# Low parts of the memories' weights moved from VectorE to GpSimd in a hybrid encoder

## The chip, the cores and the metric

One Trainium2 chip, of which the kernel uses one core. The metric is the device time of one execution in microseconds (us). The engines are named as the profile names them: PE is TensorE (PEld its weight loads), DVE is VectorE, ACT is ScalarE, POOL is GpSimd, SP is SyncE, whose queue issues the DMAs here.

## The reference

One layer of an encoder, on a prompt of 1024 tokens and a sample of 2048 tokens, each with 256 memory tokens, model width 1024, all in float32.

```python
h = rms_norm(x, norm_pre)
z = jnp.einsum('btd,de->bte', h, w_in)          # 1024 -> 2304, split into eight parts
pool_out = multiscale_pool(u_pool, pool_w, pool_scale) * silu(g_pool)
attn_out = block_self_attention(rope(rms_norm(q)), rope(rms_norm(k)), v) * silu(g_attn)
mh = rms_norm(mem, mem_norm)
kv_m = jnp.einsum('bmd,de->bme', mh, w_mem_kv)  # 1024 -> 512: keys and values of the memories
x_out = memory_attention(q_x, k_m, v_m) * silu(g_x)
y = jnp.einsum('bte,ed->btd', concatenate([pool_out, attn_out, x_out]), w_out)
return x + rms_norm(y, norm_post)
```

## The kernel before

The kernel has two stretches. In the first (about 700 us) all projections are made; in the second come the attention, the output projection and the norms, in an order of slots written out by hand. The change is in the first stretch, at its very start.

**How a product is made.** A float32 matrix is split into a high part (a copy rounded to the format that PE takes, written by ACT, line 68) and a low part (the rest, a subtraction, line 69, on DVE before the change). Each product of a 128-row chunk is three matmuls, in `product`: high by high (L548), high by low (L549) and low by high (L550), summed over eight chunks of the 1024 inputs into one PSUM tile `pz` (a ring of four). The trace prints the two operands of a matmul in either order.

**The rows.** `hT_block` takes 512 rows of the memories or of x in four tiles of 128 rows: load `x` (L508, a ring of four tiles), sum of squares on ACT (L515), the reciprocal root `rs` in two steps, a small one on DVE (L61) and a power on POOL (L63), then DVE scales the rows by `rs` and the norm's gains (L517), PE transposes them in two groups of four (L523, into `pt`, a ring of two PSUM tiles), and ACT and DVE split each group into `hT_hi` and `hT_lo` (L68, L69). A `pt` tile is free again when its `hT_lo` is written.

**The weights.** `weights` loads a piece of a weight matrix into `wraw` (L539), of which there is **one** buffer, and splits it into `w_hi` and `w_lo` (rings of two). The next piece's load can start only when both parts of the one before are written. The first three uses are: `w_mem_kv` for the memories' values in two halves of 128x1024 (tiles numbered 251 to 253 in the order listings), `w_mem_kv` for their keys, 128x2048 (260 to 262), and then the pieces of `w_in`, 128x3072 each (474 to 476, then 636 to 638).

**The groups in order.** `mem_v` (the memories' values; `pz_362` to `pz_446`), `mem_k` (their keys; `pz_480` and `pz_511`, matmuls of 128x512; the results are scaled and split on DVE and ACT into `qxst`, one buffer), then the token groups, first `group_n1` (`pz_661` and on, matmuls of 128x384, with norms and rotary positions on POOL and DVE). Before that, `rope_tables` makes four tables of 128x1024 on POOL (L595, with small copies, L587), which `group_n1` needs.

**The order of the work.** In this stretch the instructions of each engine are put in order when the program is built, by a scheduler with its own timeline; at run time each engine goes through its list in order and waits at whatever isn't ready. A change of one instruction's engine therefore moves many others in the lists, while the work stays the same.

Of the kernel before, what the change touches and what calls it, by code (L numbers as in the profile page):

```python
# [7 lines left out]
F32 = mybir.dt.float32  # L8
F32R = mybir.dt.float32r
AF = mybir.ActivationFunctionType  # L10
ALU = mybir.AluOpType
# [12 lines left out]
def encoder(ctx, tc, I, O):  # L24


    nc = tc.nc
# [35 lines left out]
        nc.gpsimd.tensor_tensor(out=r, in0=r, in1=mhalf[:, 0:n], op=ALU.pow)  # L63
        return r

    def split(hi, lo, src):

        nc.scalar.copy(out=hi, in_=src)  # L68
        nc.vector.tensor_tensor(out=lo, in0=src, in1=hi.bitcast(F32), op=ALU.subtract)  # L69


    KA, KB, V = [], [], []
# [60 lines left out]
    class Group:  # L133
# [78 lines left out]
        def weights(self, k, j):  # L212
            if j == 0:
                self.P[k] = dbl.tile([128, 2, 512], F32, name="P", tag="P", bufs=6)
            S = pss.tile([128, 512], F32, name="S", tag="S")
            keys = slice(128 * k, 128 * k + 128)
            for n, (K, q) in enumerate(((KA, self.qa[:, j]), (KB, self.qb[0:65, j]))):
                rows_ = slice(0, 128 if n == 0 else 65)
                if self.kind < 2:
                    nc.tensor.matmul(S, lhsT=K[self.kind][rows_, keys], rhs=q, start=n == 0, stop=n == 1)  # L220
                    continue
                for i in range(2):
                    x = slice(256 * i, 256 * i + 256)
                    nc.tensor.matmul(S[:, x], lhsT=K[2][rows_, i, j, keys], rhs=q[:, x],
                                     start=(n, i) == (0, 0), stop=(n, i) == (1, 1),
                                     skip_group_check=True)
            nc.scalar.activation(out=self.P[k][:, j], in_=S, func=AF.Exp)  # L227
# [209 lines left out]
    for g in groups:  # L437
        n, c = first[g], g.chunks
# [14 lines left out]
    looks, n = {}, len(slots)  # L453
# [22 lines left out]
    with ExitStack() as p1:  # L476
# [24 lines left out]
        def hT_block(sb, blk):  # L501

            kind = SB[sb][0]
            hi = big.tile([128, NC, 512], F32R, name="hT_hi", tag="hT_hi")
            lo = big.tile([128, NC, 512], F32R, name="hT_lo", tag="hT_lo")
            for i in range(4):
                x = ftwo.tile([128, D], F32, name="x", tag="x", bufs=4)
                nc.sync.dma_start(out=x, in_=rows(sb, blk, i))  # L508
                if kind not in gains:
                    gains[kind] = fone.tile([128, D], F32, name="gain", tag="gain")  # L510
                    src = I["mem_norm" if kind == "mem" else "norm_pre"]
                    nc.sync.dma_start(out=gains[kind], in_=src.broadcast_to([128, D]))
                junk = fone.tile([128, D], mybir.dt.bfloat16, name="junk", tag="junk")
                ss = ftwo.tile([128, 1], F32, name="ss", tag="ss")
                nc.scalar.activation(out=junk, in_=x, func=AF.Square, accum_out=ss)  # L515
                r = rsqrt(ftwo, ss, 1, D, "rsx")
                nc.vector.scalar_tensor_tensor(out=x, in0=x, scalar=r[:, 0:1], in1=gains[kind],  # L517
                                               op0=ALU.mult, op1=ALU.mult)
                for half in range(2):
                    pt = pst.tile([128, 4, 128], F32, name="pt", tag="pt")  # L520
                    for c in range(4):
                        cc = 4 * half + c
                        nc.tensor.transpose(out=pt[:, c], in_=x[:, 128 * cc:128 * cc + 128],  # L523
                                            identity=ident)
                    cs = slice(4 * half, 4 * half + 4)
                    split(hi[:, cs, 128 * i:128 * i + 128], lo[:, cs, 128 * i:128 * i + 128], pt)
            return hi, lo

        def weights(src, pieces, cuts=1):

            n = sum(w for _, w in pieces)
            raw = big.tile([128, NC, 384], F32, name="wraw", tag="wraw", bufs=1)
            hi = big.tile([128, NC, 384], F32R, name="w_hi", tag="w_hi")
            lo = big.tile([128, NC, 384], F32R, name="w_lo", tag="w_lo")
            for q in range(cuts):
                cs, at = slice(NC // cuts * q, NC // cuts * (q + 1)), 0
                for start, w in pieces:
                    cols = src[:, start:start + w].rearrange("(c p) f -> p c f", p=128)
                    nc.sync.dma_start(out=raw[:, cs, at:at + w], in_=cols[:, cs])  # L539
                    at += w  # L540
                split(hi[:, cs, 0:n], lo[:, cs, 0:n], raw[:, cs, 0:n])
            return hi, lo

        def product(ps, terms, beside=lambda: None):
# [93 lines left out]
        def heads_transposed(src, npair):  # L638

            pt = pst.tile([128, 4, 128], F32, name="ptq", tag="ptq")  # L640
            for c in range(npair):
                nc.tensor.transpose(out=pt[:, c], in_=src[:, 128 * c:128 * c + 128], identity=ident)
            o = ftwo.tile([128, 2, 3, 128], F32R, name="qst", tag="qst")
            split(o[:, 0, 0:npair], o[:, 1, 0:npair], pt[:, 0:npair])
            return o
# [140 lines left out]
        w_mem = I["w_mem_kv"][0]  # L786
# [27 lines left out]
        def first_weights(sb):  # L814
            src, pieces, _ = groups_of(sb)[0]
            return weights(src, pieces, cuts=2 if sb == 0 else 1)
# [6 lines left out]
        for sb, (kind, s, nb, b0) in enumerate(SB):  # L823
            groups = groups_of(sb)
            nxt = []
            for gi, (src, pieces, run) in enumerate(groups):
                w = nxt_w
                if gi + 1 < len(groups):
                    nxt_w = weights(groups[gi + 1][0], groups[gi + 1][1])
                elif sb + 1 < len(SB):  # L830
                    nxt_w = first_weights(sb + 1)
                final = gi + 1 == len(groups)
                last = sb + 1 == len(SB)
                if last and gi == 3:
                    front.close()
                    early = ctx.enter_context(tc.tile_pool(name="early", bufs=1, side="right", reuse_waits="tile"))
                    open_early()
                    for g in loads.pop(-1):
                        g.load()
                if last and gi == 3:  # L840
                    heads.close()
                    psn = ctx.enter_context(tc.tile_pool(name="psn", bufs=2, space=PSUM, side="right", reuse_waits="tile"))
                for blk in range(nb):
                    if kind == "mem" and gi == 0 and blk == 0:
                        nxt.append(hT_block(sb + 1, 0))
                    if last and final:
                        with tc.manual_schedule(engines={mybir.EngineType.PE}):
                            run(s, b0 + blk, cur[blk], w, look_ahead)
                    else:
                        run(s, b0 + blk, cur[blk], w)  # L850
                    if final and sb + 1 < len(SB) and len(nxt) < SB[sb + 1][2]:
                        nxt.append(hT_block(sb + 1, len(nxt)))
# [22 lines left out]
    with tc.manual_schedule(engines=order):  # L875
        slot = 0
        while slot < len(slots) or later or fill:
# [14 lines left out]
            n = -(-(len(fill) - pauses) // max(1, until[0] - slot - pauses)) if fill else 0  # L892
            for _ in range(n):
# [3 lines left out]
                out, h, c, start, final = x  # L897
# [57 lines left out]
```

## Time and profile before

| what | value |
|---|---|
| time, median of 3 runs (lowest to highest) | 1884.36 us (1883.71 to 1887.12) |
| the profiled execution: its own time, its span | 1885.09 us, 1883.0 us |
| PE busy | 1816.8 us, 96% of the span |
| DVE, ACT, POOL busy | 1131.4, 697.3, 856.7 us (60%, 37%, 45%) |
| DMA | 181.83 MB, mean 97 GB/s |

The span runs from the first to the last instruction of the profile; the time of the execution has 2.09 us more around it. A row of a timeline has the start and the duration in us, the engine, the line and operation, output<-inputs, the shapes, how many instructions are merged (x2), and in brackets the idle time before it with what ended it. The starts of pipelined instructions lie a little ahead of the ends of those before them.

### The profile page before, as it was taken

The page shows a single profiled execution, that of the slowest core. Times are in us where ns is not written, and L with a number is a line of the kernel's source. Part 1 is how long each engine was busy: PE and PEld are TensorE (multiplying, and loading weights), DVE is VectorE, ACT ScalarE, POOL GpSimd, SP SyncE. Part 2 cuts the span into 40 slices and gives each one's busy share as a digit, 9 for nine tenths or more (in the row PEclk, how much of TensorE's full clock was granted, in tenths as well). Part 3 has the DMA queues.
Part 4 walks back from the last instruction along what each step waited for, and adds up shares of the span by engine and source line. Part 5 has one row for each costly group of instructions (what it writes and reads, how often), then busy time and mean ns, then how long its engine had stood idle before and what let it go on. Part 6 is the DMA issues. An engine that isn't in the chain of part 4 may idle for free. (4 is left out here: it accounts for less than half of the span.)

```text
span 1883.0 us, 23531 instructions
## 1 busy us (share of the span) xinstructions
PE 1816.8 (96%) x8520; PEld 1282.0 (68%) x8520; DVE 1131.4 (60%) x1304; ACT 697.3 (37%) x1266; POOL 856.7 (45%) x756
## 2 busy tenths in 40 slices
PE   7999999999999998999999999999999999999996
PEld 6888888988988874465564656556565656565564
DVE  7755146431545167867768676767868576756743
ACT  5523233222422115434434343444434343433331
POOL 3665017520546008845638374664837461413313
PEclk9999999999999999999999999999999999999998
DMA  7634454254433926212122220212222242223211
GB/s 243 201 113 121 109 160 132 76 162 110 116 113 102 216 70 167 68 30 79 46 79 62 70 64 25 79 45 79 62 74 62 67 132 64 91 84 100 86 40 62
DMA packets 148485, 181.83 MB, mean 97 GB/s; under 512 B 21505, under 2 KB 118417, under 8 KB 148369
## 3 DMA queue, kind: packets, MB, share of 16 engines
q1 hardware_dynamic: 148368, 180.33, 33.6%
q8 instruction: 67, 1.10, 0.3%
q14 instruction: 50, 0.40, 0.1%
HBM read 126.50 MB, written 53.62 MB: 96 GB/s over the span
## 5 line engine op out<-in xcount | busy, mean ns | idle before, releaser
L227 ACT ACTIVATE P<-S 128x512 f32<-128x512 f32 x688 | 399.3, 598 | 558.3 <-PE S L220 436.2
L194 DVE TENSOR_REDUCE nb<-N 128x1 f32<-128x1024 f32 x256 | 311.6, 1218 | 240.3 <-PE N L191 239.5
L239 POOL TENSOR_TENSOR z<-z,P 128x512 f32<-128x512 f32 x224 | 316.9, 1415 | 223.7 <-ACT P L227 218.8
L252 PE MATMUL acc<-P,V 128*64 128x512 f32 (+1 forms) x1472 | 320.8, 578 | 0.5
L220 PE MATMUL S<-qa,KA 128*128 128x512 f32 x640 | 275.0, 430 | 9.2 <-ACT P L227 9.2
L240 DVE TENSOR_TENSOR z<-z,P 128x512 f32<-128x512 f32 (+1 forms) x272 | 273.6, 1006 | 12.7 <-ACT P L227 12.3
L63 POOL TENSOR_TENSOR rs<-rs,mhalf 128x1 f32<-128x1 f32 (+2 forms) x100 | 100.4, 1007 | 386.2 <-DVE rs L61 386.1
L220 PE MATMUL S<-qb,KB 65*128 65x512 f32 x640 | 254.5, 398 | 0.0
L548 PE MATMUL pz<-hT_hi,w_hi 128*128 128x512 f32 x592 | 233.2, 394 | 1.4 <-ACT vmst L806 0.8
L549 PE MATMUL pz<-hT_lo,w_hi 128*128 128x512 f32 x592 | 232.3, 392 | 0.0
L550 PE MATMUL pz<-hT_hi,w_lo 128*128 128x512 f32 x592 | 232.1, 392 | 0.2 <-DVE w_lo L69 0.2
L191 PE MATMUL N<-KA,qa 128*128 128x512 f32 x640 | 208.1, 406 | 18.4 <-DVE rz L272 11.7
L252 PEld LDWEIGHTS acc<-P,V 128*64 128x64 f32 x1472 | 98.6, 138 | 180.3 <-issue 171.2
L220 PEld LDWEIGHTS S<-qa,KA 128*128 128x128 f32 x640 | 120.4, 188 | 143.6 <-issue 72.5
L194 DVE TENSOR_REDUCE top<-N 128x1 f32<-128x1024 f32 (+1 forms) x88 | 107.0, 1218 | 96.7 <-PE N L191 76.9
L191 PEld LDWEIGHTS N<-KA,qa 128*128 128x128 f32 x640 | 116.9, 191 | 61.7 <-DVE nb L194 22.1
L548 PE MATMUL pz<-w_hi,hT_hi 128*128 128x384 f32 (+1 forms) x416 | 140.3, 338 | 1.4 <-ACT hT_hi L68 1.4
L549 PE MATMUL pz<-w_lo,hT_hi 128*128 128x384 f32 (+1 forms) x416 | 139.9, 336 | 1.0 <-DVE w_lo L69 0.9
L550 PE MATMUL pz<-w_hi,hT_lo 128*128 128x384 f32 (+1 forms) x416 | 140.1, 338 | 0.0
L357 PE MATMUL py<-wo_hi,mix 128*128 128x512 f32 x352 | 137.7, 391 | 0.0
L358 PE MATMUL py<-wo_lo,mix 128*128 128x512 f32 x352 | 137.6, 391 | 0.0
L359 PE MATMUL py<-wo_hi,mix 128*128 128x512 f32 x352 | 137.4, 390 | 0.0
(116 smaller groups left out, 2487.9 us busy)
## 6 DMA issues: line engine op xcount, KB each, us to landing
wraw<-w_in SPq DMA_DIRECT2D x15, 1536.0 KB
dg<-gst SPq DMA_DIRECT2D x48, 256.0 KB
qa<-dq SPq DMA_DIRECT2D x48, 256.0 KB
gz<-rows SPq DMA_DIRECT2D x72, 128.0 KB
x<-x_sample SPq DMA_DIRECT2D x16, 512.0 KB
xr<-x_sample SPq DMA_DIRECT2D x16, 512.0 KB
y_sample<-xr SPq DMA_DIRECT2D x16, 512.0 KB
dq<-qst SPq DMA_DIRECT2D x96, 64.0 KB
```

Of the source, the lines that this page charges most:

```text
L191: nc.tensor.matmul(S[:, 512 * b:512 * b + 512], lhsT=q, rhs=KA[self.kind][:, k:k + 512], start=True, stop=True)
L194: nc.vector.tensor_reduce(out=out, in_=S, axis=AX.X, op=ALU.max, negate=True)
L220: nc.tensor.matmul(S, lhsT=K[self.kind][rows_, keys], rhs=q, start=n == 0, stop=n == 1)
L227: nc.scalar.activation(out=self.P[k][:, j], in_=S, func=AF.Exp)
L239: nc.gpsimd.tensor_tensor(out=z[:, :cut], in0=a[:, :cut], in1=P[:, :cut], op=ALU.add)
L240: nc.vector.tensor_tensor(out=z[:, cut:], in0=a[:, cut:], in1=P[:, cut:], op=ALU.add)
L252: nc.tensor.matmul(self.acc[64 * j:64 * j + 64, x], lhsT=v, rhs=P[:, j, x], start=(k, i) == (0, 0), stop=k == self.chunks - 1, skip_group_ ...
L357: nc.tensor.matmul(ps, lhsT=mh, rhs=wo_hi[:, c, cols], start=first, stop=False)
L358: nc.tensor.matmul(ps, lhsT=mh, rhs=wo_lo[:, c, cols], start=False, stop=False)
L548: nc.tensor.matmul(ps, lhsT=sh, rhs=mh, start=c == 0, stop=False)
L549: nc.tensor.matmul(ps, lhsT=sh, rhs=ml, start=False, stop=False)
L550: nc.tensor.matmul(ps, lhsT=sl, rhs=mh, start=False, stop=c == n - 1)
```

## The change

`split` gets a parameter for the engine of the subtraction, and `weights` gives it POOL where the source is the memories' weight matrix. These are three instructions: two halves of 128x1024 and one of 128x2048. The pieces of `w_in`, all `hT_lo` and all `qxst` stay on DVE. From line 541 on the lines of the changed file are two higher (L548 to L550 become L550 to L552, L587 L589, L595 L597).

```diff
--- before.py
+++ after.py
@@ -63,10 +63,10 @@
         nc.gpsimd.tensor_tensor(out=r, in0=r, in1=mhalf[:, 0:n], op=ALU.pow)
         return r
 
-    def split(hi, lo, src):
+    def split(hi, lo, src, e=nc.vector):
 
         nc.scalar.copy(out=hi, in_=src)
-        nc.vector.tensor_tensor(out=lo, in0=src, in1=hi.bitcast(F32), op=ALU.subtract)
+        e.tensor_tensor(out=lo, in0=src, in1=hi.bitcast(F32), op=ALU.subtract)
 
 
     KA, KB, V = [], [], []
@@ -538,7 +538,9 @@
                     cols = src[:, start:start + w].rearrange("(c p) f -> p c f", p=128)
                     nc.sync.dma_start(out=raw[:, cs, at:at + w], in_=cols[:, cs])
                     at += w
-                split(hi[:, cs, 0:n], lo[:, cs, 0:n], raw[:, cs, 0:n])
+
+                split(hi[:, cs, 0:n], lo[:, cs, 0:n], raw[:, cs, 0:n],
+                      nc.gpsimd if src is w_mem else nc.vector)
             return hi, lo
 
         def product(ps, terms, beside=lambda: None):
```

The order of the lists changes as follows. **POOL**, in the first 40 us of the program: before, the power of the fourth memory tile (`rs_233`) was followed by the rope tables, and the powers of the rows of x (`rs_275` and on) lay between them.

```order
L63 TENSOR_TENSOR rs_233<-rs_233,mhalf_128 128x1
L587 COPY hg_646<-hg_646 128x2x16 x2
L595 TENSOR_TENSOR ropek_650<-ropec_642,hg_646 128x1024
L595 TENSOR_TENSOR ropek_652<-ropes_643,hg_646 128x1024
L587 COPY hg_654<-hg_654 128x2x16 x2
L595 TENSOR_TENSOR ropec_642<-ropec_642,hg_654 128x1024
L63 TENSOR_TENSOR rs_275<-rs_275,mhalf_128 128x1
L63 TENSOR_TENSOR rs_298<-rs_298,mhalf_128 128x1
L595 TENSOR_TENSOR ropes_643<-ropes_643,hg_654 128x1024
L63 TENSOR_TENSOR rs_321<-rs_321,mhalf_128 128x1
```

In the changed program the two halves (`w_lo_253`) stand around `rs_233`, ahead of the rope tables, and the 128x2048 piece (`w_lo_262`) stands behind all of them and behind the power for `x_316`:

```order
L63 TENSOR_TENSOR rs_233<-rs_233,mhalf_128 128x1
L69 TENSOR_TENSOR w_lo_253<-wraw_251,w_hi_252 128x4x256
L589 COPY hg_646<-hg_646 128x2x16 x2
L597 TENSOR_TENSOR ropek_650<-ropec_642,hg_646 128x1024
L589 COPY hg_654<-hg_654 128x2x16 x2
L597 TENSOR_TENSOR ropek_652<-ropes_643,hg_646 128x1024
L63 TENSOR_TENSOR rs_275<-rs_275,mhalf_128 128x1
L597 TENSOR_TENSOR ropec_642<-ropec_642,hg_654 128x1024
L63 TENSOR_TENSOR rs_298<-rs_298,mhalf_128 128x1
L597 TENSOR_TENSOR ropes_643<-ropes_643,hg_654 128x1024
L63 TENSOR_TENSOR rs_321<-rs_321,mhalf_128 128x1
L69 TENSOR_TENSOR w_lo_262<-wraw_260,w_hi_261 128x8x256
```

Three subtractions have joined the list, and the last stands ahead of the powers `rs_344`, `rs_549` and `rs_572`, which are next.

**PE**, where the keys of the memories begin (`pz_480`); before, one group of transposes was done by then, and the last products of the values (`pz_446`) still came between:

```order
L523 MATMUL pt_279<-ident_123,x_268 128x128 x4
L548 MATMUL pz_480<-hT_hi_155,w_hi_261 128x512
L549 MATMUL pz_480<-hT_lo_156,w_hi_261 128x512
L548 MATMUL pz_446<-w_hi_252,hT_hi_155 128x256
L549 MATMUL pz_446<-w_lo_253,hT_hi_155 128x256
L548 MATMUL pz_511<-hT_hi_155,w_hi_261 128x512
L549 MATMUL pz_511<-hT_lo_156,w_hi_261 128x512
L550 MATMUL pz_480<-hT_hi_155,w_lo_262 128x512
```

In the changed program:

```order
L523 MATMUL pt_279<-ident_123,x_268 128x128 x4
L523 MATMUL pt_286<-ident_123,x_268 128x128 x4
L550 MATMUL pz_480<-hT_hi_155,w_hi_261 128x512
L551 MATMUL pz_480<-hT_lo_156,w_hi_261 128x512
L550 MATMUL pz_511<-hT_hi_155,w_hi_261 128x512
L551 MATMUL pz_511<-hT_lo_156,w_hi_261 128x512
L523 MATMUL pt_302<-ident_123,x_293 128x128 x4
L523 MATMUL pt_309<-ident_123,x_293 128x128 x4
L523 MATMUL pt_325<-ident_123,x_316 128x128 x4
L523 MATMUL pt_332<-ident_123,x_316 128x128 x4
L552 MATMUL pz_480<-hT_hi_155,w_lo_262 128x512
```

Six groups of transposes and all of `pz_446` now stand ahead of the first matmul that reads `w_lo_262`.

**DVE**, at the scaling of the first rows of x; before:

```order
L517 SCALAR_TENSOR_TENSOR x_268<-x_268,rs_275,gain_270 128x1024
L517 SCALAR_TENSOR_TENSOR x_293<-x_293,rs_298,gain_270 128x1024
L69 TENSOR_TENSOR w_lo_262<-wraw_260,w_hi_261 128x8x256
L69 TENSOR_TENSOR hT_lo_156<-pt_244,hT_hi_155 128x4x128
L61 TENSOR_SCALAR rs_321<-ss_319 128x1
L61 TENSOR_SCALAR rs_344<-ss_342 128x1
L69 TENSOR_TENSOR hT_lo_267<-pt_279,hT_hi_266 128x4x128
L517 SCALAR_TENSOR_TENSOR x_316<-x_316,rs_321,gain_270 128x1024
L517 SCALAR_TENSOR_TENSOR x_339<-x_339,rs_344,gain_270 128x1024
```

In the changed program:

```order
L517 SCALAR_TENSOR_TENSOR x_268<-x_268,rs_275,gain_270 128x1024
L61 TENSOR_SCALAR rs_321<-ss_319 128x1
L517 SCALAR_TENSOR_TENSOR x_293<-x_293,rs_298,gain_270 128x1024
L61 TENSOR_SCALAR rs_344<-ss_342 128x1
L69 TENSOR_TENSOR hT_lo_267<-pt_279,hT_hi_266 128x4x128
L517 SCALAR_TENSOR_TENSOR x_316<-x_316,rs_321,gain_270 128x1024
L69 TENSOR_TENSOR hT_lo_267<-pt_286,hT_hi_266 128x4x128
L61 TENSOR_SCALAR rs_549<-ss_547 128x1
```

The subtraction `w_lo_262` is gone from between the scalings; `x_316` (which waits for its power on POOL) now stands ahead of the splits of the transposed rows from `pt_286` on.

## Rows read from the trace of the kernel before

**Rows 1.** The page: busy time and share of the span by engine.

```profile
PE 1816.8 (96%) x8520; PEld 1282.0 (68%) x8520; DVE 1131.4 (60%) x1304; ACT 697.3 (37%) x1266; POOL 856.7 (45%) x756
```

**Rows 2.** Waits of PE, 0 to 60 us: waiter, releaser, total, times, longest.

```profile
PE pz L550 <- DVE w_lo L69: 0.2, 1, 0.2
```

**Rows 3.** Timeline of DVE: scaling of rows, low parts of weights.

```profile
12.55 1.28 DVE L517 SCALAR_TENSOR_TENSOR x<-x,rs,gain 128x1024 f32<-128x1024 f32 x1
...
17.34 3.15 DVE L69 TENSOR_TENSOR w_lo<-wraw,w_hi 128x1024 fp32r<-128x1024 f32 x1
...
30.84 2.28 DVE L69 TENSOR_TENSOR w_lo<-wraw,w_hi 128x2048 fp32r<-128x2048 f32 x1
...
43.47 3.35 DVE L69 TENSOR_TENSOR w_lo<-wraw,w_hi 128x3072 fp32r<-128x3072 f32 x1
...
58.62 3.36 DVE L69 TENSOR_TENSOR w_lo<-wraw,w_hi 128x3072 fp32r<-128x3072 f32 x1 [2.78 <-ACT w_hi L68]
```

**Rows 4.** Timeline of ACT: high parts of the first and third weights.

```profile
12.06 1.04 ACT L68 CAST w_hi<-wraw 128x1024 fp32r<-128x1024 f32 x1
...
40.66 2.77 ACT L68 CAST w_hi<-wraw 128x3072 fp32r<-128x3072 f32 x1
```

**Rows 5.** Timeline of SP: the load issued behind the 128x2048 piece.

```profile
33.14 0.38 SPq L539 DMA_DIRECT2D wraw<-w_in  x1
```

**Rows 6.** Timeline of POOL: a power, copies, rope tables.

```profile
11.97 0.55 POOL L63 TENSOR_TENSOR rs<-rs,mhalf 128x1 f32<-128x1 f32 x1 [2.13 <-DVE rs L61]
...
16.30 0.74 POOL L587 COPY hg<-hg 128x32 f32<-128x32 f32 x2 [0.86 <-DMA hg<-k_norm]
17.00 2.41 POOL L595 TENSOR_TENSOR ropek<-ropec,hg 128x1024 f32<-128x1024 f32 x1
...
26.59 3.24 POOL L595 TENSOR_TENSOR ropes<-ropes,hg 128x1024 f32<-128x1024 f32 x1
```

**Rows 7.** Groups by form: the same subtraction on POOL, later in the kernel.

```profile
L118 POOL TENSOR_TENSOR wo_lo<-raw,wo_hi 128x1024 fp32r<-128x1024 f32 x8 | 20.6, 2575 | 6.8 <-ACT wo_hi L117 6.6
```

**Rows 8.** Timeline of POOL, then of DVE, where both want SBUF at once.

```profile
67.29 1.52 POOL L63 TENSOR_TENSOR rs<-rs,mhalf 128x4 f32<-128x4 f32 x2
68.79 1.57 POOL L625 TENSOR_TENSOR sq<-z,ropes 128x64 f32<-128x64 f32 x2
...
89.73 0.45 POOL L620 TENSOR_TENSOR t<-z,ropek 128x128 f32<-128x128 f32 x1
...
68.85 1.34 DVE L517 SCALAR_TENSOR_TENSOR x<-x,rs,gain 128x1024 f32<-128x1024 f32 x1
...
89.70 1.56 DVE L517 SCALAR_TENSOR_TENSOR x<-x,rs,gain 128x1024 f32<-128x1024 f32 x1
```

**Rows 9.** Timeline of PE: keys of the memories, first token group.

```profile
33.17 0.50 PE L550 MATMUL pz<-hT_hi,w_lo 128*128 128x512 f32 x1 [0.20 <-DVE w_lo L69]
...
36.02 0.39 PE L548 MATMUL pz<-hT_hi,w_hi 128*128 128x512 f32 x1
36.25 0.39 PE L549 MATMUL pz<-hT_lo,w_hi 128*128 128x512 f32 x1
...
38.07 1.04 PE L523 MATMUL pt<-ident,x 128*128 128x128 f32 x8
38.87 0.36 PE L550 MATMUL pz<-w_hi,hT_lo 128*128 128x256 f32 x1
...
46.88 0.44 PE L549 MATMUL pz<-w_lo,hT_hi 128*128 128x384 f32 x1
...
68.82 0.44 PE L642 MATMUL ptq<-ident,t 128*128 128x128 f32 x2 [0.51 <-DVE t L632]
...
70.84 0.66 PE L523 MATMUL pt<-ident,x 128*128 128x128 f32 x4 [0.71 <-DVE hT_lo L69]
...
77.01 0.45 PE L548 MATMUL pz<-w_hi,hT_hi 128*128 128x384 f32 x1 [1.36 <-ACT hT_hi L68]
```

**Rows 10.** Busy time by engine in a stretch, PE clock, DMA share, GB/s.

```profile
35.00:40.00 5.00, 5.00 (x32) 4.40 (x31) 3.25 (x5) 1.07 (x2) 0.00 (x0) 1.00 0.96 332
```

## The prediction

> **What bounds the kernel now.** First the page: PE is busy 96% of the span [rows 1], so time that PE loses in the first stretch is not made up behind it, unless it takes the place of a wait. Next the waits of PE at the start: for a low part of weights they show one of 0.2 us in the keys of the memories [rows 2]. The timelines say why it is so short: it is met just in time. DVE ends the 128x2048 low part `w_lo_262` at 30.84 + 2.28 = 33.12 us [rows 3], and the first matmul that reads it starts at 33.17 [rows 9]. The next piece is as close: its low part ends at 43.47 + 3.35 = 46.82 [rows 3], its first reader starts at 46.88 [rows 9]. Between the two lies a chain without slack: there is one buffer `wraw`, so the load of the next piece is issued when the low part is done (33.14, [rows 5]), the cast to the high part starts at 40.66 [rows 4], and the low part follows. PE is full over 35 to 40 us [rows 10], but what it may do next hangs on this chain. So the question is not how busy DVE is, but when `w_lo_262` is ready.
>
> **What goes and comes.** From DVE go three subtractions: 2.28 us for the large one, and by the same pace 1.1 us for each half, 4.5 us in all; the second half took 3.15 only because POOL was in a 2.41 us multiplication from 17.00 on [rows 3, 6]. On DVE they were no bound, so by themselves they give nothing. To POOL come the same three. The same subtraction to the same type took 2.58 us on POOL in the mean of eight, for 128x1024 [rows 7]; the rope multiplication of that size, alone, took 2.41, of which some 0.03 overlap with its neighbour (the copies at 16.30 + 0.74 end at 17.04, it starts at 17.00, [rows 6]). I take 2.38, the undisturbed one, and count the disturbances apart: two halves 4.76, the large one 2 x 2.38 = 4.76. At 2.58 the sum below would be 0.8 us later. No row has 128x2048 on POOL. [...]
>
> **When w_lo_262 is ready.** POOL's list puts it behind both halves, four powers, the copies and four rope tables. POOL can start the first half when its high part is there (12.06 + 1.04 = 13.10, [rows 4]), but DVE's scaling of `x_205` runs until 12.55 + 1.28 = 13.83 [rows 3], and the rows show that an operation of DVE with two inputs in SBUF and one of POOL do not run together: the 3.15 us above, and the rope table of 3.24 us at 26.59, which is 0.85 over its price [rows 6]. So from 13.83: two halves 4.76, four powers of 0.52 each (0.55 in the row, less the overlap with the next, [rows 6]) 2.1, copies 0.7 [rows 6], four rope tables 9.5, the large piece 4.76. That is 21.8, or 35.6 us. Four scalings of rows (`x_228`, `x_268`, `x_293`, `x_316`) each wait for one of these powers and come up at the moment at which POOL's next long operation does. Each costs POOL a scaling of 1.2 us (1.28 less the overlap, [rows 3]) if DVE goes first: 4.8. Together 40.4 us against 33.12: **7.3 us later**. Bounds: 35.6 with no collision at all, 41.2 with the longer price.
>
> **Who goes first there.** The nearest row is exactly such a place. The second of POOL's two powers ends at 67.29 + 1.52 = 68.81; POOL's next operation is down as started at 68.79, DVE's scaling, released by that power, at 68.85. The scaling took 1.34, about its price, and POOL's 1.57 for two small ones [rows 8]: DVE went first though it started later. The row at 89.70 speaks the other way: the scaling took 1.56, and POOL's operation at 89.73 its plain 0.45 [rows 8]; but that scaling was not released by POOL. I take DVE first. [...]
>
> **What PE loses.** The load of `w_in` is issued at 40.4. In the trace it took at most 7.5 us from issue to cast (33.14 to 40.66, [rows 4, 5]); the DMAs were already full in the 35 to 40 us stretch [rows 10] and the cast could have waited for something else, so 6.5 to 7.5: I take 7.0. From cast to low part it is 46.82 - 40.66 = 6.2. So the low part is ready at 53.6. PE by then: two groups of transposes still to come (0.8 for eight transposes, 38.07 to 38.87, so 0.4 a group) and 44 matmuls of 128x512 at 0.23 (36.02 to 36.25, [rows 9]), that is 40.4 + 0.8 + 10.1 = 51.3. It waits 2.3 us, and the first token product comes 53.6 - 46.9 = 6.7 us later. By then it has done eight groups of transposes instead of five: 1.2 us to the good, so 5.5 lost. The next load, of the second `w_in` piece, hangs on the same buffer (its low part ran from 58.62, [rows 3]) and keeps the delay, so it isn't caught up there. What can be won back are the three waits that PE has behind it: 0.51, 0.71 and 1.36, 2.6 in all [rows 9]. Two of them are for transposed rows, which are now further ahead. But the backlog of DVE behind the late pieces of `w_in` is the same; I take 1.0 of the 2.6. That leaves **+4.5 us** (from 2.4 to 6.0 with the ends of the load, 0.5 either way, and of what is won back). At the very start the first half is also later on POOL (13.83 + 2.4 = 16.2) than on DVE, but two groups of transposes have been put ahead of its first reader, so I count nothing; without that cover it would be 1.1 us.
>
> The sum is made against the profiled execution, 1885.09 us (span 1883.0 and 2.09 around it): 1889.6. The median before is 0.73 lower, so I forecast 1884.36 + 4.5 = **1888.9 us**, 0.24% slower. About 0.2%, 3.8 us, is what a measurement here can tell from no change (the three runs spread over 3.4 us).
>
> **The rivals.**
> *POOL goes first at each collision.* Then `x_316` isn't scaled before `w_lo_262` (40.4 - 1.2 = 39.2) is through, at 40.4. The split of `pt_286` stands behind it on DVE (0.6), `pt_309` behind that on PE (0.4), and on SP the load of a tile of x that needs the buffer of `pt_309` stands ahead of the load of `w_in`. That is issued at 42 or later, 1.6 us or more after the 40.4 above; with the same chain behind it, 4.5 + 1.6 = +6.1: 1890.5, or somewhat more. For it speaks the row at 89.70, against it the one at 68.85.
> *Slower by less than can be told.* PE's lead and the three waits take more of the delay: all 2.6 won back and a load of 6.5 us give 6.2 - 1.2 - 2.6 = +2.4, 1886.8. For it: the rows of x really are scaled and transposed earlier, and nothing forces DVE's backlog to cost PE. Without two of the four collisions (2.4 us less) it would be +2.1.
> *Faster: the rows of x decide.* DVE, freed of 4.5 us, has the transposed rows ready early, the three waits go (2.6), and the three groups of transposes ahead (1.2) count in full: -3.8, 1880.6. That needs `w_lo_262` at 33.1 as before, 2.5 us below even the sum without a collision. Were it at 35.6, the first token product would come at 35.6 + 7.0 + 6.2 = 48.8, 1.9 late; less 1.2 and 2.6 that is -1.9, 1882.5, which couldn't be told from no change. So it takes a POOL much faster than its rows.
> That the change does nothing is no rival: the lists show the three operations on POOL.
>
> **How the numbers follow.** The forecast, +3.8 to +6: 0.42. POOL first, or more: 0.18. Slower or same within the bound: 0.33. Faster by more: 0.07. So faster 0.07, same 0.33, slower 0.60. The likeliest's own range is 1888.2 to 1890.4. For 8 in 10 the range goes to half of the small cases below (1885) and past POOL first above (1893).
>
> **What the profile after would show.** Right: POOL's 128x1024 subtractions near 2.4 us plus what they wait; the 128x2048 one ending at 39 to 41; PE with waits for a POOL `w_lo` and then for DVE's at about 53 to 54; the waits at 68 to 77 smaller. Wrong: `w_lo_262` before 37, a first token product before 50, or later stretches that differ by more than a shift. [...]

## The result and the profile after

The changed kernel is slower: its time is 1.0028 times that of before, 95% interval 1.0021 to 1.0035, or +5.3 us (+4.0 to +6.6) on a median of 1884.87 us (18 runs of each; the changed kernel's median is 1890.47). The difference lies in the forecast's range of +3.8 to +6; the median itself is 1.6 us above the 1888.9 us of the forecast. The profiled execution has a span of 1889.3 us, against 1883.0 before.

PE is still busy nearly all the time, as in [rows 1]; the first line of the page of after, part 1:

```profile
PE 1818.8 (96%) x8520; PEld 1283.0 (68%) x8520; DVE 1132.7 (60%) x1301; ACT 697.7 (37%) x1266; POOL 867.6 (46%) x759
```

How much of the loss lies in the projections shows at the first exponential of the attention, ahead of which ACT loads a table. ACT's timeline of before, and then of after (start, duration, instruction):

```profile
699.35 1.28 ACT L227 ACT_TABLE_LOAD   x1
```

```profile
49.93 2.76 ACT L68 CAST w_hi<-wraw 128x3072 fp32r<-128x3072 f32 x1 [3.81 <-DMA wraw<-w_in]
...
704.30 1.28 ACT L227 ACT_TABLE_LOAD   x1
```

It comes 4.95 us later, so nearly all of the loss is made before it. The 1.3 us by which the spans differ beyond that lie in the attention, which the change does not touch; from this row to the end of the span the profiled executions of the kernels below differ by up to 6.0 us (1179.9 in e7, 1185.9 in e2), so 1.3 can't be told from chance. Where the 4.95 us arise is read from the timelines of the first 95 us, one engine after the other. POOL's, after:

```profile
13.26 2.78 POOL L69 TENSOR_TENSOR w_lo<-wraw,w_hi 128x1024 fp32r<-128x1024 f32 x1 [0.76 <-ACT w_hi L68]
...
16.52 2.39 POOL L69 TENSOR_TENSOR w_lo<-wraw,w_hi 128x1024 fp32r<-128x1024 f32 x1
18.85 1.35 POOL L589 COPY hg<-hg 128x32 f32<-128x32 f32 x2
...
25.89 2.39 POOL L597 TENSOR_TENSOR ropec<-ropec,hg 128x1024 f32<-128x1024 f32 x1
28.24 1.53 POOL L63 TENSOR_TENSOR rs<-rs,mhalf 128x1 f32<-128x1 f32 x1
29.74 2.37 POOL L597 TENSOR_TENSOR ropes<-ropes,hg 128x1024 f32<-128x1024 f32 x1
32.08 1.53 POOL L63 TENSOR_TENSOR rs<-rs,mhalf 128x1 f32<-128x1 f32 x1
33.58 4.51 POOL L69 TENSOR_TENSOR w_lo<-wraw,w_hi 128x2048 fp32r<-128x2048 f32 x1
```

The last row is `w_lo_262`: it ends at 38.09 us, where DVE ended it at 33.12 before [rows 3]. DVE's timeline, after:

```profile
16.58 3.40 DVE L517 SCALAR_TENSOR_TENSOR x<-x,rs,gain 128x1024 f32<-128x1024 f32 x1 [1.48 <-POOL rs L63]
...
20.51 2.11 DVE L585 TENSOR_SCALAR hg<-hg 128x64 f32<-128x64 f32 x1
...
26.25 3.12 DVE L517 SCALAR_TENSOR_TENSOR x<-x,rs,gain 128x1024 f32<-128x1024 f32 x1 [0.71 <-DMA gain<-norm_pre]
...
29.80 3.40 DVE L517 SCALAR_TENSOR_TENSOR x<-x,rs,gain 128x1024 f32<-128x1024 f32 x1 [0.18 <-POOL rs L63]
...
33.97 5.20 DVE L517 SCALAR_TENSOR_TENSOR x<-x,rs,gain 128x1024 f32<-128x1024 f32 x1
39.09 0.68 DVE L69 TENSOR_TENSOR hT_lo<-pt,hT_hi 128x512 fp32r<-128x512 f32 x1
...
52.73 3.36 DVE L69 TENSOR_TENSOR w_lo<-wraw,w_hi 128x3072 fp32r<-128x3072 f32 x1 [2.98 <-ACT w_hi L68]
```

Each of the four scalings (`x_228`, `x_268`, `x_293`, `x_316`) starts after one of POOL's long operations has started, and ends 1.1 us after that one's end: it took 3.1 to 5.2 us instead of its own 1.28. The last, `x_316`, met `w_lo_262` and was done at 39.17; the split of `pt_286`, which stands behind it in DVE's list, ended at 39.09 + 0.68 = 39.77. What hung on it shows in SP's queue, after:

```profile
40.97 0.33 SPq L508 DMA_DIRECT2D x<-x_prompt  x1
...
41.88 0.38 SPq L539 DMA_DIRECT2D wraw<-w_in  x1
...
56.12 0.38 SPq L539 DMA_DIRECT2D wraw<-w_in  x1
```

The load of a tile of x and a short store stand ahead, the first goes at 40.97; the load of `w_in` follows at 41.88, 3.8 us after the buffer was free and 8.7 us later than in [rows 5]. The cast follows at 49.93 (ACT, above), the low part at 52.73 + 3.36 = 56.09, the next load at 56.12. PE's timeline, after:

```profile
34.11 0.66 PE L523 MATMUL pt<-ident,x 128*128 128x128 f32 x4
39.83 1.97 PE L523 MATMUL pt<-ident,x 128*128 128x128 f32 x8 [5.06 <-DVE rs L61]
...
43.11 0.78 PE L552 MATMUL pz<-hT_hi,w_lo 128*128 128x512 f32 x1
...
56.14 0.44 PE L551 MATMUL pz<-w_lo,hT_hi 128*128 128x384 f32 x1 [0.85 <-DVE w_lo L69]
...
93.93 0.44 PE L644 MATMUL ptq<-ident,t 128*128 128x128 f32 x2 [0.24 <-DVE t L634]
```

PE stands idle for 5.06 us. The bracket names `rs`, the last thing on DVE before it, but what PE's list waits for is a free `pt` tile: the transposes into `pt_309` start when the split of `pt_286` is done (39.77). PE does not wait for `w_lo_262` at all: its first reader starts at 43.11, 5.0 us after the piece was ready. The first product that needs the low part of `w_in` comes at 56.14 instead of 46.88 [rows 9]: 9.3 us late. Two ways lead there and nearly tie: PE is free at 55.29 (56.14 less the wait of 0.85), the low part is ready at 56.09. Both pass through the held `x_316`; the load's ends last, by 0.8 us. Of the three waits that PE had between 68 and 78 us [rows 9] nothing is left; up to 110 us there is only the one of 0.24. The clock, in windows of after (length, busy time and count of PE, PEld, DVE, ACT and POOL, then the granted clock of PE, DMA share, GB/s):

```profile
34.80:39.80 5.00, 0.00 (x0) 0.00 (x0) 5.00 (x4) 1.89 (x4) 4.78 (x2) 0.79 0.00 1
39.80:44.40 4.60, 4.02 (x15) 3.43 (x16) 3.27 (x6) 1.76 (x3) 0.55 (x1) 0.50 0.47 147
44.40:50.00 5.60, 5.60 (x26) 4.52 (x26) 3.78 (x5) 1.48 (x4) 0.55 (x1) 0.99 1.04 384
```

In the stretch in which PE does nothing the granted clock falls (0.79 in the mean of its 5.00 us), and the 4.02 us of work behind it run at 0.50: eight transposes take 1.97 us against 1.04 in [rows 9]. That is 2.0 us of PE's time (an estimate: half of 4.02), but PE waits another 0.85 us for the low part at 56.14; at the full clock it would for the most part have waited longer there. Not wholly: the first four of those transposes (`pt_309`) free the tile that the load of x at 40.97 takes, and at the full clock they, and with them the load of `w_in`, would have come some 0.5 us sooner (an estimate: half of 1.97, against half of 1.04).

### The profile page after: what moved, and what is told of

Read it like the earlier page. It is cut to its first block, busy times and chain, and to the rows that moved or that the text cites. A ratio compares the mean times of both kernels' runs of the same rounds, so it can differ in the third digit from the quotient of the medians.

```text
span 1889.3 us, 23543 instructions
## 1 busy us (share of the span) xinstructions
PE 1818.8 (96%) x8520; PEld 1283.0 (68%) x8520; DVE 1132.7 (60%) x1301; ACT 697.7 (37%) x1266; POOL 867.6 (46%) x759
## 5 line engine op out<-in xcount | busy, mean ns | idle before, releaser
L550 PE MATMUL pz<-hT_hi,w_hi 128*128 128x512 f32 x592 | 233.3, 394 | 1.2 <-ACT vmst L808 1.1
L552 PE MATMUL pz<-hT_hi,w_lo 128*128 128x512 f32 x592 | 231.9, 392 | 0.0
L552 PE MATMUL pz<-w_hi,hT_lo 128*128 128x384 f32 (+1 forms) x416 | 139.4, 335 | 0.0
L550 PE MATMUL pz<-w_hi,hT_hi 128*128 128x384 f32 (+1 forms) x416 | 139.1, 336 | 0.0
```

The costliest lines, as they stand in the source:

```text
L550: nc.tensor.matmul(ps, lhsT=sh, rhs=mh, start=c == 0, stop=False)
L552: nc.tensor.matmul(ps, lhsT=sl, rhs=mh, start=False, stop=c == n - 1)
```

## Experiments

Two theories to begin with. **A:** the late `w_lo_262` holds the one load buffer, so the load of `w_in` and all behind it come late. **B:** the cost is POOL's hold on DVE: scalings that wait for long operations of POOL. Medians and ratios are against runs of the kernel before on the same chip in the same session. "First exp" is the row of the table load as above (before 699.35, after 704.30). It is one execution of each kernel, but free of the attention behind it, in which the executions differ by up to 6.0 us though no edit here is in it; how much the first exp itself varies from one execution to the next no row shows.

**e1: only the halves on POOL.**

```
-                      nc.gpsimd if src is w_mem else nc.vector)
+                      nc.gpsimd if src is w_mem and cuts == 2 else nc.vector)
```

> Only the two 128x1024 low parts are on POOL, the 128x2048 one (w_lo_262) is back on DVE. Theory A (the late w_lo_262 holds the single load buffer, and the load of w_in comes 8.7 us late): w_lo_262 no longer stands behind the rope tables, so its end is at 33 to 35 us and the load of w_in is issued at 33 to 35; the time is that of before, -1 to +2 us. Theory B (what costs is that DVE's scalings of the rows wait for long operations of POOL, whatever becomes of w_lo_262): the scalings x_228, x_268 and x_293 still wait for POOL (3.1 to 3.4 us each, as in the changed kernel), and the time is +3 to +5 us over before. The kernel leaves nothing out.

Measured: ratio 1.0000 (0.9991 to 1.0010), first exp at 698.79. DVE's timeline of e1, and SP's:

```profile
16.65 3.42 DVE L517 SCALAR_TENSOR_TENSOR x<-x,rs,gain 128x1024 f32<-128x1024 f32 x1 [1.48 <-DMA poolw<-pool_w]
...
26.19 3.27 DVE L517 SCALAR_TENSOR_TENSOR x<-x,rs,gain 128x1024 f32<-128x1024 f32 x1 [0.41 <-DMA gain<-norm_pre]
...
29.91 3.40 DVE L517 SCALAR_TENSOR_TENSOR x<-x,rs,gain 128x1024 f32<-128x1024 f32 x1 [0.18 <-POOL rs L63]
...
33.24 2.28 DVE L69 TENSOR_TENSOR w_lo<-wraw,w_hi 128x2048 fp32r<-128x2048 f32 x1
```

```profile
35.54 0.38 SPq L539 DMA_DIRECT2D wraw<-w_in  x1
```

Three of the four scalings wait just as in the changed kernel, and the loss is gone. So B falls as far as these three go: what they cost can't be told from nothing. The fourth meeting, of `x_316` with `w_lo_262`, is gone here together with the lateness of the piece, so e1 doesn't part the two there; e6 does. The load, issued 2.4 us later than before, costs nothing either; PE loses 0.7 us between 60 and 80 us instead of 2.6 before, so a delay of this size comes out of waits that PE has anyway.

**e2: only the 128x2048 piece on POOL** (`cuts == 1` in the line above).

> Only the 128x2048 low part is on POOL, the halves are back on DVE. POOL's list before it is shorter by two operations of 2.4 us, so by the changed kernel's rows it ends at 38.09 - 4.8, or 33.3 us, about where DVE ended it before (33.12). Theory A: the load of w_in is issued at 33 to 36 us and the time is -1 to +2 us against before, although the largest operation of the change is still on POOL. Theory B: the scaling that meets this operation still waits some 4 us for it, the rows behind it with it, and the time is +3 to +5 us. The kernel leaves nothing out.

Measured: ratio 1.0009 (0.9997 to 1.0020), first exp at 701.01. POOL starts `w_lo_262` at 29.61, waits a scaling out in it (5.55 instead of 4.51 us) and ends it at 35.16; the load goes at 35.18, the first product with the low part of `w_in` at 49.13. By its median this is A's case, though the interval reaches to B's +3.8 us. The piece was expected at 33.3 and came at 35.2.

**e5: the lateness by itself, without POOL.** The kernel before, with DVE making `w_lo_262` three times:

```
                 split(hi[:, cs, 0:n], lo[:, cs, 0:n], raw[:, cs, 0:n])
+                if src is w_mem and cuts == 1:
+                    for _ in range(2):
+                        nc.vector.tensor_tensor(out=lo[:, cs, 0:n], in0=raw[:, cs, 0:n],
+                                                in1=hi[:, cs, 0:n].bitcast(F32), op=ALU.subtract)
```

> [...] Theory A (a late w_lo_262 holds the load): the first product of tokens comes at 54 to 57 us (46.88 before) and the time is +3 to +6 us, as in the changed kernel. Theory B (POOL's hold on DVE costs): no scaling waits more than before, and the time is -1 to +2 us. The kernel leaves nothing out.

Measured: ratio 1.0040 (1.0026 to 1.0053), +7.5 us, first exp at 706.80. DVE's, SP's and PE's timelines of e5:

```profile
30.92 2.28 DVE L69 TENSOR_TENSOR w_lo<-wraw,w_hi 128x2048 fp32r<-128x2048 f32 x1
33.84 2.28 DVE L544 TENSOR_TENSOR w_lo<-wraw,w_hi 128x2048 fp32r<-128x2048 f32 x1
39.63 2.28 DVE L544 TENSOR_TENSOR w_lo<-wraw,w_hi 128x2048 fp32r<-128x2048 f32 x1
```

```profile
41.94 0.38 SPq L539 DMA_DIRECT2D wraw<-w_in  x1
```

```profile
56.75 0.44 PE L553 MATMUL pz<-w_lo,hT_hi 128*128 128x384 f32 x1 [1.83 <-DVE w_lo L69]
```

The load goes within 0.1 us of where the changed kernel's went (41.88), the first product within 0.6 us, and the whole loss is there, with POOL as it was before. So POOL's hold isn't needed for the loss. The lateness is not quite by itself: the two added subtractions are 4.6 us of work for DVE too, and the rows behind them come later. But PE waits 1.83 us for the low part of `w_in` at 56.75, so the load's way ends last here as well. That e5 loses more than the changed kernel is within the intervals; its PE had done 56 transposes by the first product, the changed kernel's 64.

**e6: POOL's low parts in small operations.**

```
+                    for c in range(cs.start, cs.stop):
+                        nc.gpsimd.tensor_tensor(out=lo[:, c, 0:n], in0=raw[:, c, 0:n],
+                                                in1=hi[:, c, 0:n].bitcast(F32), op=ALU.subtract)
```

> The changed kernel with POOL's three low parts cut into operations of 128x256 (4, 4 and 8 of them, some 0.6 us each). If the engine that is in an operation keeps the other out for just that operation, a scaling of DVE that meets them takes 2 us or less instead of 3.4 and 5.2 (those that meet rope tables still 3.1 to 3.4). Theory A: w_lo_262 ends no earlier than in the changed kernel (38 to 40 us), but the rows are let through, so the load of the x tile that stood ahead of the load of w_in is out in time and the latter is issued at 38 to 40.5 instead of 41.88: +2 to +4.5 us against before. If only the waits of the scalings for low parts mattered, it would be 0 to +1.5. The kernel leaves nothing out.

Measured: ratio 1.0020 (1.0009 to 1.0031), first exp at 703.57. DVE's, POOL's and PE's timelines of e6:

```profile
17.06 1.75 DVE L517 SCALAR_TENSOR_TENSOR x<-x,rs,gain 128x1024 f32<-128x1024 f32 x1 [1.91 <-DMA poolw<-pool_w]
...
19.34 0.18 DVE L590 TENSOR_SCALAR hg<-hg 128x64 f32<-128x64 f32 x1
...
34.11 1.74 DVE L517 SCALAR_TENSOR_TENSOR x<-x,rs,gain 128x1024 f32<-128x1024 f32 x1 [0.30 <-POOL rs L63]
```

```profile
34.04 6.57 POOL L545 TENSOR_TENSOR w_lo<-wraw,w_hi 128x256 fp32r<-128x256 f32 x8
```

```profile
50.14 0.79 PE L555 MATMUL pz<-w_hi,hT_hi 128*128 128x384 f32 x3 [2.86 <-ACT w_hi L68]
...
53.53 0.69 PE L556 MATMUL pz<-w_lo,hT_hi 128*128 128x384 f32 x1 [2.60 <-DVE w_lo L69]
```

The scalings that took 3.40 and 5.20 us take 1.75 and 1.74: the hold lasts for one operation. But `w_lo_262` ends at 40.61, as the rows now go between its pieces, and the load goes at 40.64, at once: the 3.8 us of gap are gone, 2.5 us of lateness have come in their place. By the medians that is 1.5 us under the changed kernel, with intervals that overlap: the load, 1.2 us sooner than there, again goes with the time. This run parts the two ways of the changed kernel: PE no longer stands still for rows (it is busy for 5.7 of the 6 us from 34 to 40, there for 0.8), and yet most of the loss stays, now as 2.86 and 2.60 us of waiting for the two parts of `w_in`. So the late load is enough for the loss, and the held row, which together with the low clock kept PE until 55.29 in the changed kernel, is not needed for it.

**e7: the rope tables on DVE, the change as it is** (`nc.gpsimd.tensor_tensor(out=t, in0=raw[j], ...)` of L597 on `nc.vector`).

> The changed kernel with the four rope tables on DVE (four operations of some 1.2 us there instead of 2.4 on POOL), so that nothing long stands ahead of w_lo_262 on POOL. Theory A: w_lo_262 starts when its high part is there (31.4 us in the changed kernel) and ends at 35.5 to 37.5; the load of w_in is issued at 36 to 38; +0.5 to +3 us against before, since the piece itself still takes 4.5 instead of 2.3 us. If POOL's list ahead of it isn't what makes it late: +4 us or more. The kernel leaves nothing out.

Measured: ratio 1.0014 (1.0004 to 1.0024), +2.6 us, first exp at 699.88 (the profiled execution is the fastest of the twelve, 1881.91 us; the median is 1887.55). POOL's and PE's timelines of e7:

```profile
30.82 5.07 POOL L69 TENSOR_TENSOR w_lo<-wraw,w_hi 128x2048 fp32r<-128x2048 f32 x1 [0.64 <-ACT w_hi L68]
```

```profile
35.95 0.80 PE L552 MATMUL pz<-hT_hi,w_lo 128*128 128x512 f32 x1 [2.42 <-POOL w_lo L69]
```

With nothing ahead of it the piece starts when its high part is there and still ends at 35.89, as the operation itself is 2.2 us longer on POOL (4.51 at 33.58 in the changed kernel, 2.28 on DVE [rows 3]); PE waits 2.42 us for it. The time is what A said; by the first exp the loss is only 0.5 us. Half of the change's lateness is the list ahead of the piece, half its own length.

**e8: five tiles of x instead of four** (`bufs=5`).

> The changed kernel with five buffers for tiles of x instead of four, so that no load of a tile of x waits on SP ahead of the load of w_in for a row that is still being transposed. If the 3.8 us between the end of w_lo_262 (38.09) and the issue of the load (41.88) come from there: the load is issued within 1 us of the end of w_lo_262, and the time is 1.5 to 3.5 us under the changed kernel's, +1.5 to +4 against before. If not: the gap stays at 3 us or more and the time at +4 to +6. The kernel leaves nothing out.

Measured: ratio 1.0024 (1.0013 to 1.0035), first exp at 706.50. SP's queue of e8:

```profile
42.47 0.33 SPq L508 DMA_DIRECT2D x<-x_prompt  x1
42.91 0.38 SPq L539 DMA_DIRECT2D wraw<-w_in  x1
```

The gap stays, 3.3 us from the end of `w_lo_262` at 39.59. The edit missed its aim: the scheduler, with one tile more, put one more load of x ahead of the load of `w_in`, and that one waits for the transposes of the tile five before it, which stand behind the same held scalings. What the gap is worth the run does not tell; that it comes from the held scalings, e6 shows, in which it is closed.

**e3 and e4: two buffers for loaded weights**, with the change and without it.

```
-            raw = big.tile([128, NC, 384], F32, name="wraw", tag="wraw", bufs=1)
+            raw = big.tile([128, NC, 384], F32, name="wraw", tag="wraw", bufs=2)
```

> The changed kernel with two buffers for the loaded weights instead of one, so that the load of w_in no longer waits for w_lo_262. Theory A: the load of w_in comes out 10 us or more earlier than at 41.88 us, the first product of tokens starts at 47 us or before instead of at 56.14, and the whole loss goes: 1.0 us or less above before, some us below it if the second buffer is worth something in itself (e4 tells). Theory B: scalings still wait for POOL, and the time stays +3 us or more over e4. The kernel leaves nothing out.

> The kernel before with two buffers for the loaded weights: the control of e3. The kernel before has three waits of 0.51, 0.71 and 1.36 us at 68 to 77 us and one of the order of 0.2 for weights; a second buffer may take some of them, so 0 to -3 us against before. Theory A: e3 is within 1.5 us of it. Theory B: e3 is 3 us or more above it. The kernel leaves nothing out.

Measured: e3 1.0013 (1.0003 to 1.0024), e4 0.9991 (0.9981 to 1.0001); first exp at 702.09 and 697.27. In e3 the loads of `w_in` go at 21.77 and 25.54 and the first product with its low part comes at 45.26, as early as A asked; the time does not. PE's and DVE's timelines of e3:

```profile
43.79 1.22 PE L523 MATMUL pt<-ident,x 128*128 128x128 f32 x8 [1.12 <-DVE hT_lo L69]
...
52.03 0.66 PE L523 MATMUL pt<-ident,x 128*128 128x128 f32 x4 [2.25 <-DVE hT_lo L69]
```

```profile
35.73 3.39 DVE L517 SCALAR_TENSOR_TENSOR x<-x,rs,gain 128x1024 f32<-128x1024 f32 x1 [0.44 <-POOL rs L63]
...
48.02 3.35 DVE L69 TENSOR_TENSOR w_lo<-wraw,w_hi 128x3072 fp32r<-128x3072 f32 x1
```

PE now waits for rows, which wait on DVE behind a low part that its list has put ahead of them. By the words on record this is B's outcome: e3 stands 4.1 us over e4, and all four scalings are held and take 3.4 us each (the last of them at 35.73), though the load is early. So A fits the kernel with one buffer, but it isn't all that such operations on POOL can cost: with two buffers the change costs some 4 us as well, and that the held scalings are the cause there is argued, not shown.

**e9 and e10: two buffers, and of the change only the halves, or only the 128x2048 piece** (the edits of e1 and e2).

> Two buffers for loaded weights, and of the change only the two halves on POOL. With two buffers the whole change cost 4 us or so against e4 though no load waited (e3): this and e10 ask which of its operations does it there. If the halves (they stand ahead of the rope tables and push them and the powers of the rows back by 5 us): +3 us or more over e4's time against before. If it is the 128x2048 piece ahead of the rope tables: within 1.5 us of e4. If it is only how the lists happen to come out: no telling, anywhere between -3 and +3 us against before. The kernel leaves nothing out.

> Two buffers, and of the change only the 128x2048 piece on POOL, where it comes ahead of the rope tables in this build. If that piece is what cost in e3: +3 us or more over e4. If the halves: within 1.5 us of e4. If only the lists: anywhere between -3 and +3 us against before. The kernel leaves nothing out.

Measured: 1.0000 (0.9989 to 1.0010) and 1.0002 (0.9991 to 1.0012), first exp at 700.96 and 701.36. Each stands about 2 us over e4 by the ratios, with intervals that overlap e4's; by the first exp it is 3.7 and 4.1 us, against 4.8 for e3. So whether one operation alone makes the 4 us is not settled; the lists of x loads, low parts and transposes come out differently in all four, and what the loss in e3 comes from stays open.

**e11 and e12: the rope tables on DVE without the change, with one buffer and with two.**

> The kernel before with the four rope tables on DVE, so that POOL has no operation over 0.6 us in the first 40 us and no scaling and no low part of DVE is held up (3.15 us for the second half and 4.62 for two scalings before). DVE takes on 4 x 1.2 us, and gets back some 2 + 2.2 us of waiting. By Theory A the time turns on w_lo_262: if it still ends at 33 us or up to 2 us sooner, 0 to -2.5 us against before; if the rope tables push it back on DVE, +1 to +2.5 us. The kernel leaves nothing out.

> The kernel before with two buffers for loaded weights and the rope tables on DVE: the two edits that take away a wait each. If both are worth something: -2 to -5 us against before. If PE's waits come from the rows of x, which neither brings sooner: -2 to +1, as in e4. The kernel leaves nothing out.

Measured: e11 0.9995 (0.9984 to 1.0006), load of `w_in` at 32.66, first exp at 699.13: no difference that can be told. e12 0.9980 (0.9970 to 0.9990), -3.8 us, median 1881.67, first exp at 694.69: faster than both kernels. DVE's timeline of e12:

```profile
17.18 3.42 DVE L69 TENSOR_TENSOR w_lo<-wraw,w_hi 128x1024 fp32r<-128x1024 f32 x2
...
21.11 1.22 DVE L595 TENSOR_TENSOR ropek<-ropec,hg 128x1024 f32<-128x1024 f32 x1
22.25 0.20 DVE L583 TENSOR_SCALAR hg<-hg 128x64 f32<-128x64 f32 x1
...
27.07 1.28 DVE L517 SCALAR_TENSOR_TENSOR x<-x,rs,gain 128x1024 f32<-128x1024 f32 x1
...
28.86 1.28 DVE L517 SCALAR_TENSOR_TENSOR x<-x,rs,gain 128x1024 f32<-128x1024 f32 x1
```

A rope table takes 1.22 us on DVE against 2.4 on POOL, and with nothing long on POOL every scaling of the first 50 us takes its plain 1.28 or 1.29. So the opposite of the change, work of two SBUF inputs moved to DVE, goes with a gain here, together with a load that doesn't wait for the low part. How much of it the rope tables have is not settled: the intervals of e4 and e12 overlap.

The kernels with one load buffer beside one another (times in us):

| kernel | load of `w_in` issued | first product with its low part | first exp | time against before |
|---|---|---|---|---|
| before | 33.14 | 46.88 | 699.35 | |
| e11 | 32.66 | 48.17 | 699.13 | -0.9 (-3.0 to +1.1) |
| e2 | 35.18 | 49.13 | 701.01 | +1.7 (-0.6 to +3.8) |
| e1 | 35.54 | 48.43 | 698.79 | 0.0 (-1.7 to +1.9) |
| e7 | 35.92 | 49.98 | 699.88 | +2.6 (+0.8 to +4.5) |
| e6 | 40.64 | 53.53 | 703.57 | +3.8 (+1.7 to +5.8) |
| changed | 41.88 | 56.14 | 704.30 | +5.3 (+4.0 to +6.6) |
| e5 | 41.94 | 56.75 | 706.80 | +7.5 (+4.9 to +10.0) |
| e8 | 42.91 | 56.93 | 706.50 | +4.5 (+2.5 to +6.6) |

The last column is the ratio less one, by 1885 us. Whoever issues the load by 36 us loses between nothing and 2.6 us, whoever issues it at 40 to 43 loses 3.8 to 7.5, wherever the low parts and the rope tables are made. By the first exp the two groups lie further apart: -0.6 to +1.7 us against +4.2 to +7.5.

## Why the prediction was right, and where it was not

**The bound.** Right in the main: the loss hangs on the load behind `w_lo_262`. e5 and e6 show it, and e1, e2 and e7 fit. What counted was when that load is issued, which was 3.8 us after the piece was ready.

**The price on POOL.** 2.38 us for a half was right (2.39 at 16.52). For the large piece 2 x 2.38 = 4.76 was 0.25 too much; it took 4.51.

**When the piece is ready.** Forecast 40.4, measured 38.09. The first failed step is "DVE first": at every collision with a long operation POOL went first, as the first rival had it, with starts as little as 0.06 us apart (16.52 and 16.58). What decides it there and in the row at 68.85 [rows 8], where DVE went first, no run shows. The hold lasted for the whole of POOL's operation: the four scalings here ended 1.1 us after it, and in e6, where it was cut into small ones, 1.74 us stand in place of 5.20. What the sum and the first rival both missed is what happens at the end of the hold: the scaling that waits goes next, ahead of POOL's next operation. That one pays instead: the powers at 28.24 and 32.08 took 1.53 us for the plain 0.55, the copies at 18.85 took 1.35 for 0.74. So POOL did lose about a scaling at each meeting, as the sum had it, only behind its long operation and not ahead of it. The fourth meeting came with the piece itself, and its cost fell behind the piece: 1.2 us less ahead of it than counted; the rest of the 2.3 is the 0.25 above and collisions of 0.6 to 1.0 us instead of 1.2. The sum also left out the second pair of copies, some 0.3 us the other way.

**From there to the load.** The sum issued the load when the piece was done. It went 3.8 us after, behind a load of x that waited for rows held by `x_316`: this is the chain of the first rival, which had "42 or later". The two errors cancel in part: 40.4 forecast, 41.88 measured. From load to cast it took 8.05 us instead of 7.0, from cast to low part 6.2 as forecast. The product is 9.3 us late instead of 6.7.

**What PE does meanwhile.** The sum had PE at the first token product at 51.3, to wait 2.3 us; PE was there at 55.29 and waited 0.85. Left out were three more groups of transposes on the way (1.2 us), the lower clock (2.0) and a wait for a split. The wait for a POOL `w_lo` that the profile was to show isn't there: the 5.06 us of idle time before it are for a row.

**What comes back.** Eight groups of transposes are done by then instead of five, as forecast (64 transposes against 52): 1.2 us. Of the three waits 2.3 us come back instead of 1.0: this term was sized too small. 9.3 - 1.2 - 2.3 = 5.8; the first exp shows 4.95, and the 0.8 between them are not placed. The forecast of +4.5 was 0.8 below the measured +5.3; the first rival's +6.1 was 0.8 above, and by its mechanism it was the better of the two. That +4.5 came so near is in part luck: the piece was put 2.3 us too late, the load 1.5 too early, the first product 2.6 too early, and what PE wins back 1.3 too low.

**The clock** fell to 0.50 for 4.6 us. The sum has no term for it; what it cost was hidden in the wait, but for the half microsecond (the estimate above) by which it held the load.

## What to carry to other kernels

Before work is moved to an engine that looks free, see what stands ahead of it in that engine's list, and whether its result frees a buffer: here a low part 5 us later made a load 8.7 us later, and PE, busy 96% of the time, could get back only a part of it. Where operations of two engines wait for one another, as the scalings on DVE (3.1 to 5.2 us for 1.28) and the powers on POOL (1.53 us for 0.55) did here, moving work to the slower of them (4.51 us on POOL for 2.28 on DVE) need not make room on the faster one: DVE, rid of three operations, was busy for 1132.7 us instead of 1131.4, as each meeting here cost both engines time. Two edits that can't be told from nothing alone (e4, e11) may be worth measuring together (e12).

## What the runs showed of the hardware

- The two engines went in turn: when POOL's long operation ended, the DVE scaling that waited ran (done 1.1 us later), and POOL's next operation took 1.53 us instead of 0.55 (28.24 and 32.08).
- An operation of DVE with one SBUF input and 64 columns was held as well: the `hg` scaling at 20.51 took 2.11 us while POOL made a rope table, 0.18 while POOL made small subtractions (e6) and 0.20 with POOL idle (e12).
- After 5 us without a matmul PE's granted clock was 0.50 for the next 4.6 us, and 0.99 from 44.4 us on.
